# Eight modulation blocks moved from the input projection's VectorE sums to column matmuls between the RWKV projections' matmuls, and the RWKV stage's PSUM banks reordered

## The chip, the cores and the metric

One core of a Trainium2 chip runs the whole kernel. Its engines are TensorE (PE in the rows; its weight loads are shown apart as PEld), VectorE (DVE), ScalarE (ACT), GpSimd (POOL) and SyncE (SP), which issues the transfers. Each engine runs its own program in order. The metric is the time of one execution in microseconds. The time before is 3966.14 us, the median of three runs (3945.2 to 3976.5).

## The reference, cut to what matters

A trunk of two layers works on 128 context tokens and 1024 latent tokens (1152 in all, D_MODEL 1024, float32). Each layer modulates a normalised input by a conditioning vector, projects it once for four mixers of 512 channels each, and projects their outputs back.

```python
def reference(...):
    for l in range(DEPTH):                       # for the context with c_ctx, for the latents with c
        mod = silu(c) @ w_mod[l] + b_mod[l]      # 3 * 1024 values: shift, scale, gate
        x = trunk_layer(x, mod, ...)
    y = rmsnorm(x, final_g)

def trunk_layer(x, mod, p, states, rows, rope):
    shift, scale, gate = split(mod, 3)
    h = rmsnorm(x, norm_g) * (1 + scale) + shift
    u_a, u_b, u_c, u_d = split(h @ w_in, SPLITS)
    y_a, y_b, y_c = mlstm_branch(u_a), rglru_branch(u_b), retention_branch(u_c)
    y_d = rwkv_branch(u_d)
    y = concatenate([y_a, y_b, y_c, y_d]) @ w_out
    return x + gate * y

def rwkv step(s, r, w, k, v, kk, bb):            # per head, both directions over the tokens
    s = s * w + (s @ -kk) bb^T + v k^T
    return s, s @ r
```

## The kernel before

**Stages.** Per layer: the input projection `in_proj` with three mixers (mLSTM, RG-LRU, retention) running beside it, then the RWKV stage `rw_all`, then `tail` (the last output projection, the norm of the next layer). In the profile of before they lie at 61 to 1105 us and 1151 to 1990 us for layer 0, and at 2029 to 3013 us and 3060 to 3919 us for layer 1.

**Modulation.** `mod` of one layer is 24 columns of 128 values for two tokens' conditions, in six blocks of 512 values. The first four blocks of layer 0 are made in the opening norm. The other eight (`MODS`, line 1461) are made by `modulation` (line 1109), which `in_proj` of layer 0 steps through once every few projection jobs (lines 1263 to 1273). A block loads eight 128x512 tiles `wmod`, and VectorE multiplies each by one scalar per row and adds it to `macc`, for two conditions: 16 instructions a block, 128 in all. Then eight matmuls with a column of ones sum `macc` over the partitions into a bank that the projection also uses (`pmain`), and one small VectorE instruction adds the bias. Layer 1's `in_proj` steps through none.

**The RWKV stage.** Nine units (two per channel pair, and one for the context after the sixth) each take a *period* of `rw_all` (lines 162 to 295): `rw_chain`, 16 steps in which PE and VectorE alternate on one state, in `gap` 0 to 15; beside it VectorE runs `solve(n+1)`, 62 instructions that invert small triangular blocks, whose operands and result go through DRAM (`dU`, `iU`, `dN`, `SC<-dN`); after the chain comes `mid(n+1)`, matmuls that build the next unit's operands from the solved blocks. Ahead of the first period lies a prologue: `early(0)` (decay and gate vectors, sums over heads `v<-sq`, `v<-rk`), `operands(0)`, `scores(0)` (`a<-AR,BK`, masked into `SC`), `solve(0)`, `tokens(0)`, the same up to `scores(1)` for unit 1, `drain(1)`, `mid(0)`.

**Fills.** In both prologue and periods, PE gets other matmuls between the dependent ones: the 648 `fill` matmuls of `late_proj` (RWKV's own projections of pairs 1 to 3) and `out_proj` (line 1312, `main<-yt,ow`, 128x384). `pull(x)` (line 297) adds x to a credit and takes that many; `weave(g, x)` pulls x after each step of g; `drain(1)` takes what is left of the first 96. Each fill weight tile `ow` is 256 KB and comes from a ring of `OWB` = 6 buffers. PE keeps the program order of this stage (`strict`); the other engines' orders come from the scheduler by level. SP issues the loads of the ring and the solve's transfers in one order.

**PSUM.** The stage opens the pool `mo` (two banks, for fills) first and then `rw_ps` (six banks: tag `a` two, tags `v` and `u` two each).

Of the kernel before, what the change touches and what calls it, by code (L numbers as in the profile page):

```python
# [9 lines left out]
F32 = mybir.dt.float32  # L10
# [20 lines left out]
class B:  # L31
# [130 lines left out]
    def rw_all(self, l):  # L162
# [64 lines left out]
        def weave(g, x):  # L227
            for _ in g:
                self.pull(x)
# [3 lines left out]
        weave(early(0, 3), 8)  # L233
        operands(0, 3)
        weave(scores(0, 3), 3)
        solve(0)
        weave(tokens(0), 3)
# [8 lines left out]
        for n, (p, su) in enumerate(units):  # L246
# [6 lines left out]
            for gap in range(16):  # L253
                with self.level(3):
                    next(steps)
                self.pull(rate)
                if gap == 1 and finish is not None:
                    with self.level(1):
                        self.rw_gate(finish)
                        self.rw_final(l, finish)  # L260
                    self.finished += 1
                    finish = None
                if gap == 1 and n + 1 == N:
                    with self.level(1):
                        self.rw_gate(P[p])
                if gap >= 2:
                    next(tok, None)
                if gap == 4 and n + 2 < N:
                    block(n + 2)
                    pre = early(n + 2)  # L270
                if gap in (12, 14):
                    next(pre, None)
            weave(tok, 0)
# [23 lines left out]
    def pull(self, x):  # L297

        self.credit += x
        while self.credit >= 1:  # L300
            self.credit -= 1
            next(self.fills, None)

# [805 lines left out]
    def modulation(self, l, j, pool):  # L1109


        acc = [pool.tile([128, 512], F32, tag="macc%d" % e, name="macc") for e in range(2)]
        for k in range(8):
            w = pool.tile([128, 512], F32, tag="wmod", name="wmod", bufs=2)
            self.dma(w, self.i["w_mod"][l, j][:, k])
            for e in range(2):
                if k == 0:
                    self.ts(self.v, acc[e], w, self.sc[:, k, e:e + 1], MUL)
                else:
                    self.stt(self.v, acc[e], w, self.sc[:, k, e:e + 1], acc[e], MUL, ADD)  # L1120
        yield
        ps = self.pmain()[:, 0:8].rearrange("p (i c) -> p i c", c=2)
        for i in range(4):
            for e in range(2):
                self.mm(ps[:, i, e:e + 1], acc[e][:, 128 * i:128 * i + 128], self.ones[:, 0:1])
        self.tt(self.v, self.mod[l][:, 4 * j:4 * j + 4], ps,
                self.par["bmod"][:, 24 * l + 4 * j:24 * l + 4 * j + 4, None].broadcast_to([128, 4, 2]), ADD)
# [133 lines left out]
    def in_proj(self, l, wp, sp, mp, hh, hl):  # L1261
        n = 0
        mods = [self.modulation(z, j, mp) for z, j in MODS] if l == 0 else []
# [3 lines left out]
        for t_, (kind, name, p, tiles) in enumerate(JOBS):  # L1267
            if name[:3] == "rw_" and p in LATE:
                continue
            if mods and t_ % 4 == 0:  # L1270
                next(mods[0])
            if mods and t_ % 4 == 3:
                next(mods.pop(0), None)
# [101 lines left out]
    def build(self):  # L1375
# [10 lines left out]
        for l in range(2):  # L1386
# [7 lines left out]
            with self.ph as ph:  # L1394
                P = lambda n, b=1, **kw: ph.enter_context(tc.tile_pool(name=n + "_%d" % l, bufs=b, **kw, **tw))
                wp, sp = P("w"), P("st")
                self.in_proj(l, wp, sp, P("md") if l == 0 else None, *self.h)
# [26 lines left out]
            with ExitStack() as ph:  # L1424
                P = lambda n, b=1, **kw: ph.enter_context(tc.tile_pool(name=n + "_%d" % l, bufs=b, **kw, **tw))
                self.mainps = P("mo", 2, space=PSUM)
                wp, yp, sp = P("wo", OWB), P("yo", YOB), P("so", SO)
                with tc.high_priority(offset=HP1):
                    self.rl, self.rp = P("rw_lora", **R), P("rw_pair", **R)
                    self.rt, self.rd = P("rw_tmp"), (P("rw_even"), P("rw_odd", **R))  # L1430
                    self.rps = P("rw_ps", space=PSUM)
                    self.rw_layer(l, self.load_cols(self.rl, l, ("mu", "w0", "a0", "kk", "ka", "rk"), "rw_"))
# [11 lines left out]
                self.nfill = 648  # L1444
                self.rw_all(l)
# [15 lines left out]
MODS = ((0, 4), (0, 5), (1, 0), (1, 1), (1, 2), (1, 3), (1, 4), (1, 5))  # L1461
# [164 lines left out]
```

## Time and profile before

| what | value |
|---|---|
| median of 3 runs | 3966.14 us |
| the profiled execution, its time | 3965.97 us |
| its span | 3964.1 us |
[...]
| PE busy | 3624.5 us (91%) |
| DVE busy | 2110.8 us (53%) |
| ACT, POOL busy | 1290.7 us, 1119.5 us |
| transfers | 538 MB, mean 136 GB/s |

Times in rows are microseconds from the span's start. A matmul of float32 shows as two rows ("passes") in the trace, so 648 fills are 1296 rows a layer. An "[idle before <-X]" is the time for which the engine had nothing to run, and what ended it.

### The profile page before, as it was taken

What the parts mean: (1) busy time and instruction counts of PE and PEld (TensorE: products, weight loads), DVE (VectorE), ACT (ScalarE), POOL (GpSimd) and SP (SyncE); (2) the same over time, 40 slices, a digit from 0 to 9 for tenths busy, and PEclk for the clock granted to TensorE, in tenths of its full rate; (3) what the DMA queues carried; (4) which work ended last, traced back from release to release, by engine and by line L of the source; (5) the groups of instructions that cost most, each with busy time, mean ns of one, the idle gap of its engine ahead of it and who ended that gap; (6) DMA issues with size and microseconds to landing.
All of it is one profiled execution on the core that took longest, in us unless ns stands there. A gap on an engine that the chain in (4) does not pass through costs nothing. (4 is left out here: it accounts for less than half of the span.)

```text
span 3964.1 us, 69608 instructions
## 1 busy us (share of the span) xinstructions
PE 3624.5 (91%) x28018; PEld 2850.2 (72%) x28018; DVE 2110.8 (53%) x4081; ACT 1290.7 (33%) x2094; POOL 1119.5 (28%) x1016
## 2 busy tenths in 40 slices
PE   5898999999978999899888999999998889988997
PEld 2897888999955656555568898999996555555554
DVE  6555656433336576667264545443423556776644
ACT  3233342212222343343142344322222234343313
POOL 4222323453331122211033232344243312122200
PEclk7898898999979999899989899999897999999999
DMA  6545354434335454434663343434333444434446
GB/s 229 147 119 138 114 151 135 136 122 136 121 99 156 132 162 112 116 120 127 186 210 112 105 136 122 127 119 144 109 122 127 131 148 137 134 104 121 125 138 201
DMA packets 413549, 538.00 MB, mean 136 GB/s; under 512 B 141708, under 2 KB 322700, under 8 KB 413228
## 3 DMA queue, kind: packets, MB, share of 16 engines
q1 hardware_dynamic: 413228, 533.57, 44.7%
q8 instruction: 220, 3.60, 0.4%
q14 instruction: 101, 0.83, 0.1%
HBM read 387.17 MB, written 146.25 MB: 135 GB/s over the span
## 5 line engine op out<-in xcount | busy, mean ns | idle before, releaser
L1312 PE MATMUL main<-yt,ow 128*128 128x384 f32 x2592 | 990.5, 520 | 21.3 <-DVE xi L48 17.4
L1312 PEld LDWEIGHTS main<-yt,ow 128*128 128x128 f32 x2592 | 476.0, 197 | 316.6 <-issue 45.5
L59 PE MATMUL main<-hh,wring_h 128*128 128x384 f32 x1824 | 654.7, 359 | 22.8 <-ACT hh L56 9.8
L59 PE MATMUL main<-hl,wring_h 128*128 128x384 f32 x1824 | 648.1, 355 | 20.2 <-DVE hl L44 17.6
L59 PE MATMUL main<-hh,wring_l 128*128 128x384 f32 x1824 | 647.7, 355 | 0.0
L44 POOL TENSOR_TENSOR wring_l<-raw,wring_h 128x1024 fp32r<-128x1024 f32 x100 | 249.9, 2504 | 571.2 <-ACT wring_h L1258 428.9
L59 PEld LDWEIGHTS main<-hh,wring_h 128*128 128x128 f32 x1824 | 363.1, 199 | 38.5 <-ACT hh L56 10.3
L59 PEld LDWEIGHTS main<-hl,wring_h 128*128 128x128 f32 x1824 | 362.9, 199 | 33.6 <-DVE hl L44 21.5
L59 PEld LDWEIGHTS main<-hh,wring_l 128*128 128x128 f32 x1824 | 362.6, 199 | 8.2 <-issue 2.0
L59 PE MATMUL main<-wring_h,hh 128*128 128x256 f32 x864 | 265.0, 307 | 25.7 <-DVE st L1306 25.0
L59 PE MATMUL main<-wring_l,hh 128*128 128x256 f32 x864 | 261.0, 302 | 0.0
L59 PE MATMUL main<-wring_h,hl 128*128 128x256 f32 x864 | 259.2, 300 | 0.0
L44 DVE TENSOR_TENSOR iN<-iN,tm 64x31 f32<-64x31 f32 (+15 forms) x558 | 201.5, 361 | 15.4
L44 DVE TENSOR_TENSOR tm<-iU,iN 64x31 f32<-64x31 f32 (+15 forms) x558 | 201.1, 360 | 15.1
L1306 DVE COPY st<-main 128x384 f32<-128x384 f32 (+1 forms) x168 | 85.8, 511 | 219.8 <-PE main L59 178.4
L59 PEld LDWEIGHTS main<-wring_h,hh 128*128 128x128 f32 x864 | 178.0, 206 | 32.0 <-DVE st L1306 26.1
L44 POOL TENSOR_TENSOR t<-s_k,bb 128x512 f32<-128x512 f32 x36 | 63.3, 1758 | 465.7 <-ACT bb L56 465.7
L59 PEld LDWEIGHTS main<-wring_h,hl 128*128 128x128 f32 x864 | 177.6, 206 | 4.0 <-issue 1.1
L59 PEld LDWEIGHTS main<-wring_l,hh 128*128 128x128 f32 x864 | 177.7, 206 | 2.7
L1258 ACT CAST wring_h<-raw 128x1024 fp32r<-128x1024 f32 x100 | 103.4, 1045 | 199.7 <-PE main L59 174.4
L1304 ACT COPY st<-main 128x384 f32<-128x384 f32 (+1 forms) x168 | 73.6, 438 | 270.6 <-PE main L59 259.9
L56 ACT ACT_TABLE_LOAD x123 | 157.8, 1283 | 3.0 <-PEq L1618 0.7
(331 smaller groups left out, 6104.0 us busy)
## 6 DMA issues: line engine op xcount, KB each, us to landing
raw<-in_w_in SPq DMA_DIRECT2D x100, 512.0 KB, 4.1
ow<-in_w_in SPq DMA_DIRECT2D x144, 256.0 KB, 3.6
ow<-in_w_out SPq DMA_DIRECT2D x144, 256.0 KB, 2.7
yt<-h SPq DMA_DIRECT2D x144, 192.0 KB, 4.5
mrb<-mlrow SPq DMA_DIRECT2D x48, 384.0 KB, 4.1
x<-xi SPq DMA_DIRECT2D x96, 192.0 KB, 2.9
yt<-y SPq DMA_DIRECT2D x90, 192.0 KB, 3.2
wmod<-in_w_mod SPq DMA_DIRECT2D x64, 256.0 KB, 3.7
```

Source lines behind the costliest of these rows:

```text
L44: return e.tensor_tensor(out=out, in0=a, in1=b, op=op)
L56: return self.a.activation(out=out, in_=a, func=f, scale=scale, bias=bias)
L59: return self.t.matmul(out, l, r, start=start, stop=stop)
L1258: self.a.copy(hi, raw)
L1304: self.a.copy(q[:, :w], ps[:, :w])
L1306: self.v.tensor_copy(q[:, :w], ps[:, :w])
L1312: return self.pe(self.t.matmul(*a, **k))
```

## The change

**The modulation.** `in_proj` of layer 0 steps through no modulation any more, and its pool for `wmod` and `macc` is gone. In layer 0's RWKV stage, in four of the nine periods (1, 3, 6 and 7), `modulation` makes two blocks: each 128x128 piece of `wmod` is the stationary operand, the two conditions' `silu_c` (128x2) are the moving one, and PE accumulates over the eight k in one PSUM tile of tag `v`. That is 64 matmuls a period, 256 in all. From gap 4 on each fill that is pulled is followed by two of them; what is left runs after gap 15. Two small VectorE instructions a period add the bias. The tiles `wmod` take buffers of the ring `ow`.

**The prologue, in both layers.** No fills are woven into `early(0)` (before 8 a step), one a step into `scores(0)` (before 3), and 20 are pulled after `solve(0)`.

**The banks.** `mo` is opened behind `rw_ps`: `rw_ps` takes banks 0 to 5 and `mo` banks 6 and 7.

```diff
@@ rw_all
-        weave(early(0, 3), 8)
+        weave(early(0, 3), 0)
         operands(0, 3)
-        weave(scores(0, 3), 3)
+        weave(scores(0, 3), 1)
         solve(0)
+        self.pull(20)
         weave(tokens(0), 3)
...
+                if gap == 4 and l == 0 and n in MODS:
+                    self.beside = self.modulation(MODS[n], self.wp)
+            for _ in self.beside:
+                pass
             weave(tok, 0)
@@ pull
             next(self.fills, None)
+            next(self.beside, None)
@@ modulation
-    def modulation(self, l, j, pool):
-        acc = [pool.tile([128, 512], F32, tag="macc%d" % e, name="macc") for e in range(2)]
...
+    def modulation(self, blocks, pool):
+        ps = self.pst2("v")[:, :, 0:8].rearrange("p b (i c) -> p b i c", c=2)
         for k in range(8):
...
+            for z, (l, j) in enumerate(blocks):
+                w = pool.tile([128, 1, 512], F32, tag="ow", name="wmod")
+                self.dma(w, self.i["w_mod"][l, j][:, k:k + 1])
+                for i in range(4):
+                    self.pm(ps[:, z, i], w[:, 0, 128 * i:128 * i + 128], self.sc[:, k], start=(k + i == 0), stop=(4 * k + i == 31))
+                    if i % 2:
+                        yield
...
@@ in_proj
-        mods = [self.modulation(z, j, mp) for z, j in MODS] if l == 0 else []
...
-            if mods and t_ % 4 == 0:
-                next(mods[0])
-            if mods and t_ % 4 == 3:
-                next(mods.pop(0), None)
@@ build
-                self.mainps = P("mo", 2, space=PSUM)
                 wp, yp, sp = P("wo", OWB), P("yo", YOB), P("so", SO)
...
                     self.rps = P("rw_ps", space=PSUM)
+                    self.mainps = P("mo", 2, space=PSUM)
@@ numbers
-MODS = ((0, 4), (0, 5), (1, 0), (1, 1), (1, 2), (1, 3), (1, 4), (1, 5))
+MODS = {1: ((0, 4), (0, 5)), 3: ((1, 0), (1, 1)), 6: ((1, 2), (1, 3)), 7: ((1, 4), (1, 5))}
```

**PE in the prologue.** Before, PE's program in layer 0's prologue runs from the second `lora` step through the head sums and the first scores like this:

```order
L59 MATMUL a<-lora_x,lora_w 128x512 x2
L59 MATMUL v<-sq,bones 128x512
L1312 MATMUL main<-yt,ow 128x384 x8
L59 MATMUL v<-rk,bones 128x512 x2
L59 MATMUL a<-AR,BK 128x128 x8
L1312 MATMUL main<-yt,ow 128x384 x3
L59 MATMUL a<-AR,BK 128x128 x8
L1312 MATMUL main<-yt,ow 128x384 x3
L59 MATMUL a<-AR,BK 128x128 x8
```

In the change the same stretch reads as follows, up to the fourth group of scores and the fills behind it:

```order
L59 MATMUL a<-lora_x,lora_w 128x512 x2
L59 MATMUL v<-sq,bones 128x512
L59 MATMUL v<-rk,bones 128x512 x2
L59 MATMUL a<-AR,BK 128x128 x8
L1310 MATMUL main<-yt,ow 128x384
L59 MATMUL a<-AR,BK 128x128 x8
L1310 MATMUL main<-yt,ow 128x384
L59 MATMUL a<-AR,BK 128x128 x8
L1310 MATMUL main<-yt,ow 128x384
L59 MATMUL a<-AR,BK 128x128 x8
L1310 MATMUL main<-yt,ow 128x384 x21
```

The 16 fills of the two `early` steps (eight stand just ahead of the first row as well) and six of the nine between the scores are gone from here; 21 stand behind the last scores. The last stretch of fills, ahead of `mid(0)`, has 29 now and had 25.

**DVE at the end of `solve(1)`.** VectorE runs the solve's pairs (`tm`, `iN`) and, among them, `mid(0)`'s copies out of PSUM (`UV<-u`), on which the chain's first step waits. Before, the end of `solve(1)` reads:

```order
L44 TENSOR_TENSOR tm<-iU,iN 64x156
L44 TENSOR_TENSOR iN<-iN,tm 64x6x26
L582 COPY UV<-u 64x4x128
L44 TENSOR_TENSOR tm<-iU,iN 64x135
L44 TENSOR_TENSOR iN<-iN,tm 64x5x27
L44 TENSOR_TENSOR tm<-iU,iN 64x112
L582 COPY UV<-u 64x4x128
L44 TENSOR_TENSOR iN<-iN,tm 64x4x28
```

In the change the same part of VectorE's program is:

```order
L44 TENSOR_TENSOR iN<-iN,tm 64x4x28
L44 TENSOR_TENSOR tm<-iU,iN 64x87
L44 TENSOR_TENSOR iN<-iN,tm 64x3x29
L44 TENSOR_TENSOR tm<-iU,iN 64x60
L44 TENSOR_TENSOR iN<-iN,tm 64x2x30
L44 TENSOR_TENSOR tm<-iU,iN 64x31
L44 TENSOR_TENSOR iN<-iN,tm 64x31
L588 COPY UV<-u 64x4x128 x2
```

Both copies stand behind the solve's last instruction now; ten and seven of its instructions stood behind them before.

**PE in a period with modulation.** In the change, PE's program in gaps 4 to 6 of period 1 is this (in before the fills there stand three together):

```order
L1310 MATMUL main<-yt,ow 128x384
L59 MATMUL v<-silu_c,wmod 128x2 x2
L59 MATMUL a<-UV,SC 64x64 x16
L59 MATMUL u<-ST,AR 64x64 x4
L1310 MATMUL main<-yt,ow 128x384
L59 MATMUL v<-silu_c,wmod 128x2 x2
L1310 MATMUL main<-yt,ow 128x384
L59 MATMUL v<-silu_c,wmod 128x2 x2
L62 MATMUL a<-ident,BK 128x128 x4
L59 MATMUL u<-UV,BT 64x64 x4
```

The `x2` are two of the 256 new matmuls, with no instruction of the chain moved past another.

## Rows read from the trace of the kernel before

**Rows 1.** The page: busy time of each engine over the span.
```profile
PE 3624.5 (91%) x28018; PEld 2850.2 (72%) x28018; DVE 2110.8 (53%) x4081; ACT 1290.7 (33%) x2094; POOL 1119.5 (28%) x1016
```

**Rows 2.** The first and last projection matmul of each layer, by start, in the timeline.
```profile
60.60 0.69 PE L59 MATMUL main<-hh,wring_h 128*128 128x384 f32 x1 [6.09 <-ACT hh L56]
...
1103.09 0.33 PE L59 MATMUL main<-hh,wring_h 128*128 128x384 f32 x1
...
2028.91 0.34 PE L59 MATMUL main<-hh,wring_h 128*128 128x384 f32 x1
...
3012.86 0.33 PE L59 MATMUL main<-hh,wring_h 128*128 128x384 f32 x1
```

**Rows 3.** Busy time by engine between them; after POOL: clock, DMA share, GB/s.
```profile
60.60:1103.10 1042.50, 974.31 (x5674) 911.33 (x5675) 533.56 (x798) 309.22 (x447) 381.06 (x350) 0.90 0.44 131
2028.90:3012.90 984.00, 937.28 (x5561) 877.14 (x5561) 445.79 (x665) 317.32 (x460) 361.77 (x348) 0.94 0.42 124
```

**Rows 4.** The tile macc: duration in ns (least, median, most), starts.
```profile
L59 PE MATMUL main<-ones,macc x128: 166/250/353, 128.0 to 834.9; 128*128 128x1 f32 x128
L48 DVE SCALAR_TENSOR_TENSOR macc<-wmod,silu_c,macc x112: 730/746/2866, 39.7 to 765.9; 128x512 f32<-128x512 f32 x112
```

**Rows 5.** The timeline around the opening norm's last steps on DVE.
```profile
55.48 1.40 DVE L48 SCALAR_TENSOR_TENSOR macc<-wmod,silu_c,macc 128x512 f32<-128x512 f32 x2
56.80 0.17 DVE L52 TENSOR_SCALAR sg<-mod 128x16 f32<-128x16 f32 x1
```

**Rows 6.** One block's ones matmuls, and fills in period 6, in PE's timeline.
```profile
127.97 1.84 PE L59 MATMUL main<-ones,macc 128*128 128x1 f32 x16
...
1800.23 2.20 PE L1312 MATMUL main<-yt,ow 128*128 128x384 f32 x6
1802.36 0.34 PE L59 MATMUL u<-ST,AR 64*64 64x64 f32 x8
```

**Rows 7.** The page: the fills' matmuls and weight loads in both layers.
```profile
L1312 PE MATMUL main<-yt,ow 128*128 128x384 f32 x2592 | 990.5, 520 | 21.3 <-DVE xi L48 17.4
L1312 PEld LDWEIGHTS main<-yt,ow 128*128 128x128 f32 x2592 | 476.0, 197 | 316.6 <-issue 45.5
```

**Rows 8.** Chains of periods 1, 3, 6 and 7 as stretches, columns of rows 3.
```profile
1355.90:1414.40 58.50, 56.95 (x498) 35.51 (x494) 39.71 (x108) 19.64 (x36) 8.49 (x7) 0.94 0.47 136
...
sum 224.80, PE 218.87 PEld 136.21 DVE 161.15 ACT 81.54 POOL 33.33; mean PE 54.72 PEld 34.05 DVE 40.29 ACT 20.39 POOL 8.33
```

**Rows 9.** PE's timeline right behind the chain of period 6.
```profile
1818.58 0.45 PE L59 MATMUL v<-ident,SC 32*32 32x32 f32 x4 [1.03 <-DMA SC<-dN]
1821.07 0.24 PE L59 MATMUL v<-ident,SC 32*32 32x32 f32 x2 [2.04 <-DMA SC<-dN]
```

**Rows 10.** SP's timeline late in period 1, and the page's line on wmod.
```profile
1399.99 0.33 SPq L81 DMA_DIRECT2D dN<-iN  x1
...
1403.87 3.78 SPq L81 DMA_DIRECT2D SC<-dN  x8
...
wmod<-in_w_mod SPq DMA_DIRECT2D x64, 256.0 KB, 3.7
```

**Rows 11.** PE's timeline in the prologues, layer 0 and (last row) layer 1.
```profile
1155.04 5.77 PE L1312 MATMUL main<-yt,ow 128*128 128x384 f32 x16
...
1161.81 1.12 PE L59 MATMUL v<-sq,bones 128*128 128x512 f32 x2
...
1174.91 0.79 PE L59 MATMUL a<-AR,BK 64*128 64x128 f32 x2 [2.06 <-POOL BK L44]
...
1284.16 0.49 PE L59 MATMUL u<-ST,AR 64*64 64x64 f32 x8 [10.14 <-DVE UV L582]
...
3192.96 0.49 PE L59 MATMUL u<-ST,AR 64*64 64x64 f32 x8 [9.32 <-DVE UV L582]
```

**Rows 12.** DVE's timeline at solve(1), layer 0.
```profile
1260.00 0.91 DVE L514 MEMSET iN<- 64x1024 f32 x1 [13.49 <-ACT iU L513]
...
1283.32 0.69 DVE L582 COPY UV<-u 64x512 f32<-64x512 f32 x1
```

More of the change, by code (lines that the diff above doesn't have):

```diff
@@ L1107, in mod_rows @@
                 self.par["bmod"][:, 24 * l + 4 * j:24 * l + 4 * j + 4, None].broadcast_to([128, 4, 2]), ADD)
-    def modulation(self, l, j, pool):
-        acc = [pool.tile([128, 512], F32, tag="macc%d" % e, name="macc") for e in range(2)]
+    def modulation(self, blocks, pool):
+        ps = self.pst2("v")[:, :, 0:8].rearrange("p b (i c) -> p b i c", c=2)
         for k in range(8):
[L1114 to L1127, printed above, removed]
+            for z, (l, j) in enumerate(blocks):
[5 more added lines that the diff above has]
+                        yield
+        for z, (l, j) in enumerate(blocks):
+            self.tt(self.v, self.mod[l][:, 4 * j:4 * j + 4], ps[:, z],
+                    self.par["bmod"][:, 24 * l + 4 * j:24 * l + 4 * j + 4, None].broadcast_to([128, 4, 2]), ADD)
     def modulation0(self, pool, ps, between):
@@ L1259, in split_w, with in_proj @@
         self.tt(self.g, lo, raw, hi.bitcast(F32), SUB)
-    def in_proj(self, l, wp, sp, mp, hh, hl):
+    def in_proj(self, l, wp, sp, hh, hl):
         n = 0
-        mods = [self.modulation(z, j, mp) for z, j in MODS] if l == 0 else []
         rh = wp.tile([128, 3, KT, 128], F32R, name="wring_h")
@@ L1396, in build @@
                 wp, sp = P("w"), P("st")
-                self.in_proj(l, wp, sp, P("md") if l == 0 else None, *self.h)
+                self.in_proj(l, wp, sp, *self.h)
                 with tc.high_priority(offset=HP1), ExitStack() as st:
@@ L1444, in build @@
                 self.nfill = 648
+                self.beside, self.wp = iter(()), wp
                 self.rw_all(l)
```

## The prediction

> **What bounds the kernel now.** I read the page first, then the stretches of each stage, then the timeline where the change touches it. PE is busy 3624.5 us of the 3964.1 [rows 1], so in nearly every stage work that leaves PE or a wait that ends on PE is worth its length, and work on another engine is worth only what PE waits for it. What the reader should see next is that the kernel brings its own control for the largest part of the change. `in_proj` runs twice on the same shapes, with modulation beside it in layer 0 and without it in layer 1. From the first projection matmul to the last, layer 0 needs 1103.09 − 60.60 = 1042.5 us, and layer 1 needs 3012.86 − 2028.91 = 984.0 us [rows 2]. So the same projection and the same three mixers cost 58.5 us more where the modulation runs.
>
> The busy times say where the 58.5 us lie [rows 3]. DVE is busy 87.8 us more in layer 0 (533.56 against 445.79), and the 16 instructions a block explain it: 112 of them take 746 ns each in the median, some far more [rows 4]. PE is busy 37.0 us more (974.31 against 937.28), and idle 21.5 us more (68.2 against 46.7). Of the 37.0 us, 128 passes with a column of ones at 1.84/16 = 0.115 us [rows 6] are 14.7 us; I give the rest to the clock, whose mean grant is 0.90 against 0.94 [rows 3].
>
> The RWKV stage is the other place. Its periods 1, 3, 6 and 7, into which the modulation goes, have chains of 224.8 us together, and PE is busy in 218.9 us of them [rows 8]. There are 5.9 us in which added PE work could disappear.
>
> **Part 1, what in_proj gives back.** The PE order of layer 0's projection in the change is that of its layer 1, apart from a few per mille of the instructions, and every mixer's instruction stands where layer 1 of before has it, within a few places. So I take layer 1 as the forecast for layer 0: −58 us. Bounds: −45, if some 13 of the 22 us (37.0 − 14.7) by which layer 0's PE is busy longer without the passes have another cause and stay; −66, if the bank that the ones matmuls held had cost a little more in layer 0 than layer 1 shows. In the opening norm the last `macc` pair ends only as `sg`, on which the first projection waits, starts at 56.80 [rows 5]; that pair's 1.4 us go too: −1, at most −5 for the pairs ahead of it.
>
> **Part 2, the column matmuls.** 256 matmuls are 512 passes, each with a new 128x128 weight tile and two columns streamed. The nearest row is the ones matmul: same weight tile, one column, 0.115 us a pass [rows 6]. 512 × 0.115 = 59 us; start to start inside the run is nearer 0.112, hence +57. From above: 0.250 us, the median duration of one such pass [rows 4], gives 128 us, but that duration overlaps with its neighbours', so I take it as no more than an outer end and use 70 (a fill's own wait on the weight that follows). From below: a fill's weight load takes 197 ns, and all of them lie beneath 520 ns matmuls [rows 7]; between two fills one of four new loads can lie beneath the fill ahead and one fill's load beneath the new ones, so a quarter may vanish: +43.
>
> The row says that the pass is bound by loading its weights. [...]
>
> What hides of the +57: the 5.9 us of idle time in the four chains [rows 8], and 3.1 us behind period 6, where `mid` waits for the solved blocks `SC<-dN` [rows 9], which a longer chain makes ready in time. I take −7 of these 9.
>
> Then new waits. The 64 loads of 256 KB move with the work. Each takes one of six ring buffers which the fills' weights had alone; a load landed in 3.7 us [rows 10]. In a period the ring now turns over about 26 tiles (16 `wmod`, some 10 `ow`) in some 72 us, 2.8 us each, so six buffers look about 14 us ahead, enough for 3.7. But SP issues in order: in the change, nine of period 1's 16 `wmod` loads stand ahead of the solve's result `dN<-iN` and seven behind it and behind the eight `SC<-dN`. In before, those were issued at 1399.99 and until 1407.65, that is 44 to 52 us after the chain began at 1355.9 [rows 8, 10]. The tenth tile would land near 1408 + 3.7, 56 us after the start. PE reaches that tile in gap 12: 13 of the 16 gaps, about 44 of the 58.5 us, and 18 pairs of new matmuls ahead of it (18 × 0.45 = 8 us) make 52 us after the start. The solve may end a little earlier because fewer chain steps are mixed into it now. So I expect some 2 us of waiting in each of four periods: +8. Bounds 0, and +35 if each of the seven late loads of each period costs PE about 1.2 us.
>
> The eight small additions on DVE count as nothing: layer 0's `out_proj` and `tail` read `mod` periods later, and PE waits for none of them.
>
> **Part 3, the prologues.** The fills leave `early(0)`. Before, 16 passes (5.77 us) stood between the two `lora` steps, so the second `v<-sq` came at 1161.81; the branch through ACT, DVE and POOL to the first `a<-AR,BK` then took until 1174.91, 13.1 us [rows 11]. Without the fills that branch starts about 5 us earlier, at 1157, and AR,BK at about 1170. But PE now has nothing in these 13 us except three pairs of head sums (3.4 us), and one fill between the scores where there were three: it idles some 9 us there. By `drain(1)` the same 96 fills must be done in both kernels, so PE reaches the end of the drain later by the added idle time, about 8 us. Of that, four fills' worth (8 passes at 0.36 us [rows 6], 2.9 us) have moved behind `scores(1)`, which so comes 5 us later.
>
> The chain starts with `u<-ST,AR`, which waits 10.14 us for a copy `UV<-u` on DVE [rows 11]. This is what ends last, not PE's fills: DVE had waited 13.49 us for the solve's operands until 1260.00, and the copy at 1283.32 stands among the solve's last instructions [rows 12]. Solve(1) follows scores(1), so the 5 us reach it in full. And both copies now stand behind all of the solve, ten and seven instructions later, about 2 us. So the chain starts 7 us later. Layer 1's prologue has the same wait, 9.32 us [rows 11], and the same edit. Both: +14. From below: if the earlier scores(0) also let everything behind it come earlier, the 5 us of fills return and it is 0. From above, if nothing starts earlier for want of fills, PE idles 13.1 − 3.4 us and some 1.4 us between each two scores, 14 a layer: +28.
>
> **Part 4, the banks.** The first PE instructions of the stage stand behind the same nine retention transposes as before, and no instruction changes its place. 0; the retention's last reads, which release the banks, cover it. Uncovered it would be one fill's wait, about a microsecond a layer.
>
> **The sum.** −58 − 1 + 57 − 7 + 8 + 14 + 0 = +13 us, against the profiled execution's 3965.97 us: 3979. That execution is within 0.2 us of the median of the runs, 3966.14, so it stands for both.
>
> **The rivals.**
>
> *The column matmuls hide, faster.* If a pass with two columns slides beneath its neighbours, as all the fills' weight loads do [rows 7], the 512 passes cost little more than a quarter, 15 us, and the sum is −29: 3937. With prologues that cost nothing, −43: 3923. For it: the fills' weight loads overlap. Against it: the run of 16 ones passes at 0.115 us, where the streaming was as short as here and nothing overlapped [rows 6]. Chance 0.15, of which 0.1 beyond 3926, where the prologues help too. [...]
>
> *SP's order holds the ring, slower.* If PE comes to the tenth `wmod` tile with its load still behind `SC<-dN`, it stops, the chain's step behind it stops, and every later fill waits for a ring buffer too. The point from which it decides: the solve's result issued later than some 45 us after the chain's start, about where it stands now (44) [rows 8, 10]. The price: in each of the four periods the wait until landing, up to 8 us, plus a landing of 3.7 us less 1.9 us of work for six further tiles, 11 us; 4 × 19 − 8 = 68 more than I count, at worst 3979 + 68 = 4047; half of it 4013. For it: loads on one queue with a wait for DVE ahead. Against it: 3.7 us to land, and the solve has fewer chain steps in it. Chance 0.2 for over 4006.
>
> *Nothing moves.* −58 and +57 cancel, the ring keeps up and the prologues cost nothing: 3966 − 9 = 3957. This lies in my range and within 1%. Chance 0.2; my forecast as summed, 0.45.
>
> **How the numbers follow.** 1% is 40 us, about what a measurement of this kernel can tell from no change (its three runs lie 31 us apart). The forecast and "nothing moves" are within 1%; so is half of the slower rival's beginning. Faster by over 1% (below 3926) 0.1, plus 0.02 for a larger gain in `in_proj` than its control shows: 0.12. Slower by over 1% (above 4006): 0.2. Within: 0.68. All lower bounds together are −66 − 5 + 43 − 9 = −37, all upper ones −45 − 1 + 70 − 4 + 35 + 28 = +83: 3929 to 4049. The range leaves out the outer part of the two rivals, a tenth on either side: 3940 to 4022. The likeliest case alone is 3960 to 3995.
>
> **What would show it.** In the profile after: layer 0's projection should take 984 ± 6 us from first to last matmul, with DVE busy near 446 us in it. Periods 1, 3, 6 and 7 should be 12 to 17 us longer and the other five the same; pairs `v<-silu_c,wmod` should stand 0.45 us a pair. Waits of PE for `wmod` in the timeline beyond 10 us in total would show the SP rival, passes under 0.06 us the faster one. `u<-ST,AR` of each layer should start 5 to 9 us later after the stage's first `lora`, still behind a `UV` copy; if it starts earlier, my step on DVE's order is wrong.

## The result

The changed kernel takes 3995.59 us, the median of seven runs (3988.65 to 4006.41), against 3960.91 us of before in the same count (3945.2 to 3976.5). The ratio is 1.0098 with a 95% interval of 1.0073 to 1.0124: 1% slower, 35 us, at the edge of what the prediction called "within 1%". The time lies inside the prediction's range of 3940 to 4022 us and 17 us above its 3979, but its sum of +13 us was too small by more than half of what came.

The profile of the change has a span of 4001.0 us, at a mean granted clock of 0.924 of full speed (0.923 in before's). Its busy line, beside [rows 1]:

```profile
PE 3674.1 (92%) x28402; PEld 2895.8 (72%) x28402; DVE 2000.3 (50%) x3953; ACT 1290.3 (32%) x2094; POOL 1096.0 (27%) x1016
```

PE gained 50 us of busy time, and DVE lost 110. The first and last projection matmul of each layer, in PE's timeline of the change, answer to [rows 2]:

```profile
56.45 0.69 PE L59 MATMUL main<-hh,wring_h 128*128 128x384 f32 x1 [4.04 <-ACT hh L56]
...
1045.00 0.33 PE L59 MATMUL main<-hh,wring_h 128*128 128x384 f32 x1
...
2076.72 0.63 PE L59 MATMUL main<-hh,wring_h 128*128 128x384 f32 x1
...
3044.83 0.33 PE L59 MATMUL main<-hh,wring_h 128*128 128x384 f32 x1
```

The busy times of (nearly) these two stretches, columns as in [rows 3]: span, PE, PEld, DVE, ACT, POOL, granted clock, DMA share, GB/s.

```profile
56.45:1046.70 990.25, 936.21 (x5560) 877.22 (x5560) 443.94 (x674) 308.86 (x448) 365.21 (x350) 0.93 0.40 123
2076.70:3046.50 969.80, 934.75 (x5596) 875.58 (x5595) 438.98 (x682) 318.88 (x466) 361.86 (x349) 0.95 0.41 127
```

And the chains of periods 1, 3, 6 and 7 as stretches, beside [rows 8]:

```profile
1299.00:1388.00 89.00, 84.99 (x625) 60.74 (x622) 41.38 (x114) 21.11 (x40) 12.09 (x12) 0.79 0.45 137
1483.70:1562.00 78.30, 72.61 (x626) 51.52 (x622) 43.12 (x116) 19.78 (x37) 9.31 (x8) 0.93 0.51 150
1759.30:1838.50 79.20, 77.74 (x576) 55.30 (x572) 44.55 (x110) 26.64 (x50) 14.13 (x14) 0.87 0.56 169
1852.40:1933.80 81.40, 76.42 (x630) 56.40 (x626) 40.65 (x110) 18.13 (x28) 5.75 (x4) 0.87 0.48 142
sum 327.90, PE 311.77 PEld 223.95 DVE 169.69 ACT 85.67 POOL 41.27; mean PE 77.94 PEld 55.99 DVE 42.42 ACT 21.42 POOL 10.32
```

The four chains take 327.9 us where they took 224.8: +103.1 us. Cut at these and a few more marks of PE's timelines (first `lora`, last chain matmul), the two profiled executions differ like this:

| stretch | before, us | change, us | difference | forecast |
|---|---|---|---|---|
| to the first projection matmul | 60.6 | 56.5 | −4.1 | −1 |
| projection of layer 0, first to last | 1042.5 | 988.6 | −53.9 | −58 |
| RWKV of layer 0, first `lora` to last chain matmul | 807.0 | 904.8 | +97.8 | +65 |
| from there to layer 1's first projection matmul | 71.2 | 78.3 | +7.1 | 0 |
| projection of layer 1, first to last | 984.0 | 968.1 | −15.9 | 0 |
| first `lora` of layer 1 to the end | 903.9 | 907.7 | +3.8 | +7 |
| the two stretches between projection and `lora` | 95.0 | 97.1 | +2.1 | 0 |

They add up to +36.9 us, the difference of the spans. So the step on `in_proj` came out, the step on the column matmuls was too small by a third of what came, and layer 1's projection, which the prediction had at zero, came out shorter. Each column is one execution, and layer 1's projection differs by up to 27 us between kernels with one and the same PE order (below).

**Where the 103 us come from.** In period 1 fills and pairs of column matmuls follow each other like this, at first and later (PE's timeline of the change; its first row is an earlier wait):

```profile
1303.30 1.70 PE L59 MATMUL a<-AR,BK 64*128 64x128 f32 x16 [1.49 <-DVE SC L44]
...
1321.69 0.89 PE L1310 MATMUL main<-yt,ow 128*128 128x384 f32 x2
1322.42 0.50 PE L59 MATMUL v<-silu_c,wmod 128*128 128x2 f32 x4
1322.78 0.89 PE L1310 MATMUL main<-yt,ow 128*128 128x384 f32 x2
...
1350.96 0.61 PE L59 MATMUL v<-silu_c,wmod 128*128 128x2 f32 x4 [2.46 <-DMA wmod<-in_w_mod]
...
1367.06 1.65 PE L1310 MATMUL main<-yt,ow 128*128 128x384 f32 x2
1368.50 0.85 PE L59 MATMUL v<-silu_c,wmod 128*128 128x2 f32 x4
1369.21 1.63 PE L1310 MATMUL main<-yt,ow 128*128 128x384 f32 x2
```

From fill to fill it is 1.09 us at first, of which the fill alone would take 0.71 [rows 6]. Between the two stands a wait of 2.46 us for a `wmod` load, and behind it fill to fill is 2.15 us. Two stretches of the same length, ahead of the wait and behind it, say why:

```profile
1321.30:1350.90 29.60, 27.20 (x245) 20.84 (x243) 17.56 (x55) 8.48 (x15) 0.00 (x0) 1.00 0.54 158
1352.00:1381.60 29.60, 29.60 (x98) 19.99 (x97) 7.77 (x14) 5.74 (x11) 5.72 (x5) 0.51 0.38 125
```

The granted clock is 1.00 ahead of the wait and 0.51 behind it, and PE is busy there without a gap. In all the lower clock stays for 34 us, past the modulation's last pass. Behind the 1.49 us wait at 1303.30, among scores and fills, it was gone after some 3 us (0.50 from 1305 to 1308 us, 1.00 from 1309). The other three periods have one wait for `wmod` each (PE's timeline of the change):

```profile
1537.82 0.61 PE L59 MATMUL v<-silu_c,wmod 128*128 128x2 f32 x4 [2.06 <-DMA wmod<-in_w_mod]
...
1816.35 0.64 PE L59 MATMUL v<-silu_c,wmod 128*128 128x2 f32 x4 [1.46 <-DMA wmod<-in_w_mod]
...
1910.26 0.61 PE L59 MATMUL v<-silu_c,wmod 128*128 128x2 f32 x4 [2.23 <-DMA wmod<-in_w_mod]
```

Behind these waits stand three stretches at the lower clock. The second row here is the rest of period 3's modulation:

```profile
1540.30:1547.10 6.80, 6.80 (x26) 3.98 (x25) 0.65 (x3) 1.27 (x2) 0.00 (x0) 0.50 0.25 77
1547.20:1557.80 10.60, 10.60 (x67) 7.76 (x66) 6.49 (x11) 3.13 (x6) 3.96 (x4) 1.00 0.50 161
1816.80:1837.20 20.40, 20.40 (x118) 14.75 (x119) 7.71 (x16) 3.04 (x7) 8.10 (x8) 0.50 0.62 196
1912.40:1932.80 20.40, 20.40 (x155) 16.46 (x154) 1.29 (x6) 0.00 (x0) 0.00 (x0) 0.50 0.34 101
```

They last 7, 20 and 20 us, which makes 82 us in the four periods. In period 3 the clock was back while two-column passes still ran, behind a group of `lora` matmuls of 512 columns; in periods 1 and 6 such a group did not bring it back, so what ends the lower clock is not shown. Nor does every wait of this size bring it: period 2's chain, without modulation, has waits of 1.51 and 1.60 us for VectorE at a clock of 1.00. At the lower clock, fill to fill takes twice as long (2.15 us against 1.09), so half of the 82 us is lost, 41 us. The waits are 8.2 us. The 54 us that are left of the 103 are near the 57 that the prediction had for the passes.

### The profile page after: what moved, and what is told of

Its sections match the earlier page's. It is cut to its first block, busy times and chain, and to the rows that moved or that the text cites. A ratio compares the mean times of both kernels' runs of the same rounds, so it can differ in the third digit from the quotient of the medians.

```text
span 4001.0 us, 70206 instructions
## 1 busy us (share of the span) xinstructions
PE 3674.1 (92%) x28402; PEld 2895.8 (72%) x28402; DVE 2000.3 (50%) x3953; ACT 1290.3 (32%) x2094; POOL 1096.0 (27%) x1016
## 5 line engine op out<-in xcount | busy, mean ns | idle before, releaser
L1310 PE MATMUL main<-yt,ow 128*128 128x384 f32 x2592 | 1027.5, 530 | 23.6 <-DVE xi L48 20.3
L44 DVE TENSOR_TENSOR tm<-iU,iN 64x31 f32<-64x31 f32 (+15 forms) x558 | 197.7, 354 | 15.9
L44 DVE TENSOR_TENSOR iN<-iN,tm 64x31 f32<-64x31 f32 (+15 forms) x558 | 193.7, 347 | 16.1
```

Source lines behind the costliest of these rows:

```text
L44: return e.tensor_tensor(out=out, in0=a, in1=b, op=op)
L1310: return self.pe(self.t.matmul(*a, **k))
```

## The experiments

The theory after this reading: the waits for `wmod` are as small as forecast, but each makes the clock fall, and the thin passes (those with two columns) that follow keep it down until the modulation of that period ends; period 3 fits this only in part. All runs, against the runs of before on the same chip:

| kernel | median, us | ratio to before | 95% interval |
|---|---|---|---|
| modulation alone | 4006.7 | 1.0108 | 1.0060 to 1.0156 |
| prologues alone | 3988.2 | 1.0065 | 1.0043 to 1.0087 |
| banks alone | 3958.8 | 0.9986 | 0.9969 to 1.0003 |
| prologues and banks | 3972.1 | 1.0036 | 1.0018 to 1.0055 |
| the change without the modulation's work | 3911.9 | 0.9872 | 0.9823 to 0.9921 |
| the change, 128 columns a pass | 3968.8 | 1.0024 | 1.0002 to 1.0046 |
| the change, one block a period | 3978.3 | 1.0054 | 1.0032 to 1.0077 |
| the change, periods 0, 2, 4, 5 | 4020.9 | 1.0167 | 1.0127 to 1.0207 |
| 128 columns, prologues of before, banks last | 3954.2 | 0.9980 | 0.9964 to 0.9996 |
| the same, blocks spread to period 8 | 3950.9 | 0.9984 | 0.9964 to 1.0004 |

### The three parts alone

Modulation alone, with the old prologues and bank order:

```diff
-        weave(early(0, 3), 0)
+        weave(early(0, 3), 8)
...
-        weave(scores(0, 3), 1)
+        weave(scores(0, 3), 3)
         solve(0)
-        self.pull(20)
...
+                self.mainps = P("mo", 2, space=PSUM)
                 wp, yp, sp = P("wo", OWB), P("yo", YOB), P("so", SO)
...
-                    self.mainps = P("mo", 2, space=PSUM)
```

> Only the modulation moves, as in the change; the prologues keep 8 and 3 fills a step and the fills' banks stay first. Theory (the column matmuls cost some 52 us of passes, 8 us of waits for wmod behind the solve's transfers, and some 40 us because PE's granted clock falls behind each of these waits and stays low; prologues and banks cost about nothing): the time is that of the whole change, 3985 to 4005 us, and chains 1, 3, 6 and 7 take 78 to 89 us each. Rival (a part of the 40 us comes from the bank order or the prologue's fills, which shift what stands in those periods): 3950 to 3980 us, with these chains near 70 us.

It is 1.08% slower, as the whole change or more. A part of that is a wait in layer 1's projection (read under the next run), so the chains say more: they take 72.8, 92.1, 78.0 and 84.3 us, 327.2 us in all against 327.9 in the change, with two of them outside the 78 to 89 us. So neither the bank order nor the prologues make the 40 us. One of its periods is a control that nobody planned. In period 1 PE waited only 0.45 us for `wmod` in this run, and in period 3 it waited 3.61 us. PE's timeline at both:

```profile
1353.94 0.61 PE L59 MATMUL v<-silu_c,wmod 128*128 128x2 f32 x4 [0.45 <-DMA wmod<-in_w_mod]
...
1525.27 0.61 PE L59 MATMUL v<-silu_c,wmod 128*128 128x2 f32 x4 [3.61 <-DMA wmod<-in_w_mod]
```

The modulation's whole stretch in period 1, and the stretch behind the wait in period 3, as windows with the granted clock after POOL:

```profile
1323.80:1368.10 44.30, 43.85 (x355) 32.83 (x353) 25.00 (x69) 13.31 (x24) 3.95 (x4) 1.00 0.64 191
1526.20:1555.90 29.70, 29.70 (x97) 19.92 (x98) 8.60 (x16) 5.26 (x10) 5.60 (x5) 0.51 0.29 89
```

In period 1 the clock stayed at 1.00 through all 128 thin passes, and the chain took 72.8 us, 14.3 more than before: the price that the prediction had for one period (57/4). In period 3 it was 92 us. So the passes as such did not lower the clock; with a wait of 3.61 us among them it fell to 0.51.

The prologues alone:

```diff
-        weave(early(0, 3), 8)
+        weave(early(0, 3), 0)
...
-        weave(scores(0, 3), 3)
+        weave(scores(0, 3), 1)
         solve(0)
+        self.pull(20)
```

> Only the prologues change (no fills in early(0), one a step in scores(0), 20 behind solve(0)), in both layers; modulation and banks as before. The prediction's step: +14 us, the chain of each layer starting 7 us later. Theory now: the chain starts 6 us later but its first period is 4 to 6 us shorter, since the solve no longer stands among the chain's first steps on DVE; +3 us in all, -3 to +8.

26 us slower in paired runs by ratio (the interval is 17 to 34), more than either forecast, and the profile puts little of it in the prologues: from the first `lora` to the end of the first chain 192.7 us against 191.0 in layer 0, 192.3 against 189.9 in layer 1. But layer 1's projection takes 1009.2 us where it took 985.6 (to the last projection pass), and a wait stands in it that before does not have:

```profile
2348.80 0.69 PE L59 MATMUL mup<-mV,mkw 128*128 128x65 f32 x2 [6.69 <-DMA mV<-ut_ml_vo]
```

The kernel with the modulation alone has layer 1's projection in the same PE order instruction by instruction, and there too PE waits 6.78 us at this place, with 17 us at the lower clock behind it, in a projection of 1002.8 us. None of the other kernels here has that order or that wait.

The banks alone:

```diff
-                self.mainps = P("mo", 2, space=PSUM)
                 wp, yp, sp = P("wo", OWB), P("yo", YOB), P("so", SO)
...
                     self.rps = P("rw_ps", space=PSUM)
+                    self.mainps = P("mo", 2, space=PSUM)
```

> Only the bank order changes: rw_ps in banks 0 to 5, the fills' pool in 6 and 7. The prediction's step: 0 us. Rival: layer 0's stretch from the last chain matmul to layer 1's first projection matmul, 71.2 us before and 78.3 us in the change, is longer by some 7 us because of the banks, and the time is 5 to 10 us above before.

No difference that can be told from zero. The rival on layer 0's tail is not borne out by the time, though that stretch is 76.7 us here; it is 74.9 to 81.0 us in every variant, those with the old bank order too, so 71.2 us in before's one profile says little. What the banks do is elsewhere: with them last, PE's order in layer 1's projection is another one than in before.

### Prologues and banks together

Both of the last two diffs.

> The prologue and the bank order of the change together, with the modulation as before. Theory: the prologue alone cost 26 us almost wholly in layer 1's input projection, where PE comes to mup before its reloaded operand (a wait of 6.7 us and 17 us of half clock in its profile); with the banks last the scheduler puts mup some 22 projection matmuls later there, the wait is gone, and the time is that of before: 3955 to 3972 us. Rival (the cost is the prologue's own, in its own stage): 3980 to 3990 us.

3972 us, at the upper end of the theory's range. Layer 1's projection takes 977.4 us, and the wait for `mV` is gone. The time is 16 us below the prologues alone by medians, which come from two chips, and 11 us by the ratios to before (1.0036 against 1.0065), whose intervals overlap. So by the ratios some 11 of the 26 us went with the wait, less than half. Between this kernel and the banks alone there remain 13 us by medians and 20 by ratios (1.0036 against 0.9986) that no single stretch shows.

The reason that the expectation gave falls, too. In the trace `mup` stands at projection matmul 1210 of the layer with the wait and at 1206 to 1212 in the runs without it, not 22 earlier; what differs is the load, which landed 12 us after its issue where 7.5 us or less sufficed in before (issued at 2326.3, `mup` at 2333.8 without a wait). Why it took so long stays open. Layer 1's projection alone varies from 967.6 us (the kernel with 128 columns a pass) to 994.4 us (one block a period) between kernels with one and the same PE order. The granted clock makes most of that: 21 of the 27 us are PE's busy time for the same matmuls, at a mean clock of 0.96 in the shorter and 0.93 in the longer.

### The change without the modulation's work

```diff
                 if gap == 4 and l == 0 and n in MODS:
-                    self.beside = self.modulation(MODS[n], self.wp)
+                    for l_, j_ in MODS[n]:
+                        self.v.tensor_copy(self.mod[l_][:, 4 * j_:4 * j_ + 4], self.par["bmod"][:, 24 * l_ + 4 * j_:24 * l_ + 4 * j_ + 4, None].broadcast_to([128, 4, 2]))
```

> The change without its column matmuls and without their 64 loads; the eight blocks of the modulation then hold the bias alone, so that part of the computation is left out. By the theory (the modulation costs about 100 us in the four periods) 3895 us, 3885 to 3910. By the prediction's price (57 us of passes, 8 of waits, 7 hidden) 3938 us. Chains 1, 3, 6 and 7 should be those of before, 55 to 59 us each.

3912 us by median: between the two forecasts and nearer to the theory's. The chains take 58.5, 60.1, 57.2 and 56.2 us, 232 us in all, so the modulation's work adds 96 us to them. In time, the modulation in the four periods costs 3995.6 − 3911.9 = 84 us by medians, or 1.0098 − 0.9872 = 0.0226 of 3961, 90 us, by the ratios. The prediction's price was 58 (57 − 7 + 8).

### More columns in the same passes

The moving operand is read 64 times over (stride zero), so that each pass streams 128 columns in place of two; weights, loads, places on PE and the count of passes stay.

```diff
-        ps = self.pst2("v")[:, :, 0:8].rearrange("p b (i c) -> p b i c", c=2)
+        ps = self.pst2("v").rearrange("p b (i x c) -> p b i x c", x=64, c=2)
...
-                    self.pm(ps[:, z, i], w[:, 0, 128 * i:128 * i + 128], self.sc[:, k], start=...)
+                    self.pm(ps[:, z, i], w[:, 0, 128 * i:128 * i + 128], self.sc[:, k, None].broadcast_to([128, 64, 2]), start=...)
...
-            self.tt(self.v, self.mod[l][:, 4 * j:4 * j + 4], ps[:, z],
+            self.tt(self.v, self.mod[l][:, 4 * j:4 * j + 4], ps[:, z, :, 0],
```

> The change, but each column matmul streams its two conditions 64 times over (128 columns into 128 PSUM columns, of which two are read): same weights, same loads, same places on PE and SP. Theory (a wait for wmod makes the granted clock fall, and the thin passes that follow keep it down to the end of the modulation): the waits of 1.5 to 2.5 us stay, the clock is back within some 7 us behind them, a pass still costs its weight load, and chains 1, 3, 6 and 7 take 70 to 78 us: 3955 to 3975 us. Rival (the clock stays low for as long whatever streams, or the wider passes cost more than they give back): 3990 us or more, half clock for 20 us and more behind each wait.

27 us below the change, though each pass does 64 times the streaming. PE's timeline of this kernel in period 1, ahead of the wait and behind it:

```profile
1323.88 0.81 PE L1310 MATMUL main<-yt,ow 128*128 128x384 f32 x2
1324.53 0.61 PE L59 MATMUL v<-silu_c,wmod 128*128 128x128 f32 x4
1324.97 0.81 PE L1310 MATMUL main<-yt,ow 128*128 128x384 f32 x2
...
1352.77 0.71 PE L59 MATMUL v<-silu_c,wmod 128*128 128x128 f32 x4 [1.76 <-DMA wmod<-in_w_mod]
1353.41 0.35 PE L59 MATMUL u<-ST,AR 64*64 64x64 f32 x8
1353.68 1.55 PE L1310 MATMUL main<-yt,ow 128*128 128x384 f32 x2
1355.03 1.06 PE L59 MATMUL v<-silu_c,wmod 128*128 128x128 f32 x4
1355.88 1.48 PE L1310 MATMUL main<-yt,ow 128*128 128x384 f32 x2
1357.16 0.65 PE L59 MATMUL v<-silu_c,wmod 128*128 128x128 f32 x4
1357.65 0.81 PE L1310 MATMUL main<-yt,ow 128*128 128x384 f32 x2
```

From fill to fill it is 1.09 us, as with two columns, (1.09 − 0.71)/4 = 0.095 us for each pass: the streaming adds nothing that shows. Behind a wait of 1.76 us the clock falls here too, but it is back some 4 us later, with the fill at 0.81 us again. The four chains as stretches:

```profile
1300.90:1376.00 75.10, 71.73 (x624) 51.25 (x620) 41.60 (x114) 21.09 (x40) 8.59 (x8) 0.95 0.55 164
1473.30:1550.10 76.80, 70.20 (x625) 50.20 (x620) 43.23 (x118) 19.76 (x37) 8.63 (x8) 0.98 0.52 153
1744.60:1816.30 71.70, 69.66 (x576) 49.00 (x570) 44.80 (x110) 26.63 (x50) 12.54 (x11) 1.00 0.62 187
1830.20:1904.60 74.40, 68.17 (x630) 49.39 (x624) 40.52 (x110) 18.12 (x28) 5.75 (x4) 1.00 0.54 155
sum 298.00, PE 279.76 PEld 199.83 DVE 170.15 ACT 85.59 POOL 35.51; mean PE 69.94 PEld 49.96 DVE 42.54 ACT 21.40 POOL 8.88
```

298.0 us against 327.9 of the change, with clocks of 0.95 to 1.00 against 0.79 to 0.93. PE waits for loads a little longer in all (1.76, 3.14, 2.04 and 3.02 us in the four, the last two in pieces of at most 1.05 and 1.71 us). Behind these waits the lower clock came in periods 1 and 3 alone, for 3.4 us each, 7 us where the change had 82. So the waits by themselves did not cost the 41 us; it took passes that stream only two columns. The run changes the passes ahead of a wait as well as those behind it, so it does not tell whether the thin passes only kept the clock down, as in the theory, or also helped it to fall. What remains above before, 73 us, is passes and waits, close to the prediction's 57 + 8.

### One block a period

```diff
-MODS = {1: ((0, 4), (0, 5)), 3: ((1, 0), (1, 1)), 6: ((1, 2), (1, 3)), 7: ((1, 4), (1, 5))}
+MODS = {1: ((0, 4),), 2: ((0, 5),), 3: ((1, 0),), 4: ((1, 1),), 5: ((1, 2),), 6: ((1, 3),), 7: ((1, 4),), 8: ((1, 5),)}
```

> The change with one block of modulation in each of the periods 1 to 8 in place of two in 1, 3, 6 and 7: the same matmuls and loads in all, eight loads a period. Theory: nearly all loads now stand ahead of the solve's transfers on SP, PE waits less than 1 us for wmod in most periods, the clock does not fall there, and the modulation costs some 50 us less what idle time it finds in periods 2, 4 and 5: 3940 to 3965 us. Rival (the thin passes lower the clock without any wait): 3985 to 4000 us as in the change.

3978 us: faster than the change, slower than expected, and both halves of that can be read. In periods 1, 3, 6 and 7 PE waited for no `wmod`, the clock did not fall at the modulation, and the chains took 63.6, 67.9, 61.4 and 62.6 us, 31 us in all above before for four blocks. In periods 2, 4 and 5 the new matmuls do not start on time, and for a reason the expectation had left out: PE stands at them and at the head sums ahead of them, which want the same PSUM tag `v`.

```profile
1399.10 1.13 PE L59 MATMUL v<-sq,bones 128*128 128x512 f32 x2 [1.83 <-DVE rn L52]
1401.01 2.03 PE L59 MATMUL v<-rk,bones 128*128 128x512 f32 x2 [0.78 <-DVE rn L52]
1403.82 2.08 PE L59 MATMUL v<-rk,bones 128*128 128x512 f32 x2 [0.78 <-DVE bs L44]
1406.68 1.01 PE L59 MATMUL v<-silu_c,wmod 128*128 128x2 f32 x4 [0.78 <-DVE bs L44]
```

These head sums (`block(n + 2)` makes them where a new pair begins) stand in periods that the change avoids. The clock then falls ahead of the thin passes (two passes of `v<-rk` take 2.03 and 2.08 us in these rows, two of `v<-sq` 1.13) and stays down for up to 30 us (chain 2: 88.9 us against 65.2).

### The periods with idle time

```diff
-MODS = {1: ((0, 4), (0, 5)), 3: ((1, 0), (1, 1)), 6: ((1, 2), (1, 3)), 7: ((1, 4), (1, 5))}
+MODS = {0: ((0, 4), (0, 5)), 2: ((1, 0), (1, 1)), 4: ((1, 2), (1, 3)), 5: ((1, 4), (1, 5))}
```

> The change with its two blocks a period in periods 0, 2, 4 and 5, whose chains left PE idle for 11.0, 3.9, 10.2 and 6.9 us before, in place of 1, 3, 6 and 7. Theory: up to 20 us of the passes hide in that idle time, but the loads still stand behind the solve's transfers, so the waits and the lower clock behind them remain in some periods: 3965 to 3990 us. Rival (the idle time is not usable, since the chain waits for DVE and the added passes only make its next step later): 3995 us as the change.

4021 us, the slowest of all, beyond both forecasts. These are the same head-sum periods, now with twice the passes in them: the chain of period 4 takes 122.8 us (78.3 before), with 24 us at the lower clock from the head sums on, a 3.86 us wait for `wmod`, and 48 us more at the lower clock behind it. Here the idle time of a chain was no room for thin passes: it sits among waits, and the clock fell at these.

### Two better versions

With 128 columns a pass, the banks last and the old prologues (the edit against the kernel with 128 columns):

```diff
-        weave(early(0, 3), 0)
+        weave(early(0, 3), 8)
...
-        weave(scores(0, 3), 1)
+        weave(scores(0, 3), 3)
         solve(0)
-        self.pull(20)
```

> The change with 128 streamed columns a pass, as in e_wide, and with the prologues of before (8 and 3 fills a step); the fills' banks stay last. Theory (the prologue costs 10 to 20 us also with the banks last, as the pair of runs with and without it showed: 3972 against 3959 us): e_wide's 3969 us less that, 3948 to 3960 us, level with before or a little faster. Rival (the prologue costs nothing once the banks are last, and what those two runs differ by is chance): 3964 to 3972 us.

3954 us, 0.2% faster than before with an interval that just leaves out 1, and 15 us below the kernel with the new prologues: the theory's case, so the new prologues cost some 15 us even with the banks last (17 by the ratios). Then with the blocks spread (the edit against the last one):

```diff
-MODS = {1: ((0, 4), (0, 5)), 3: ((1, 0), (1, 1)), 6: ((1, 2), (1, 3)), 7: ((1, 4), (1, 5))}
+MODS = {1: ((0, 4), (0, 5)), 3: ((1, 0),), 6: ((1, 1),), 7: ((1, 2), (1, 3)), 8: ((1, 4), (1, 5))}
```

> As e_wide_old, with one block of modulation in periods 3 and 6, and the two freed blocks in period 8, behind which no solve stands: {1: 2, 3: 1, 6: 1, 7: 2, 8: 2} blocks. Theory: with eight loads a period PE waited for no wmod in periods 3 and 6, and in period 8 no solve holds SP, so some 4 us of waits go: 3942 to 3956 us. Rival (period 8 has no slack and ends the stage, so its passes come out in full while the waits were worth nothing): 3952 to 3962 us.

3951 us, not to be told from the last one. Periods 3 and 6 showed no wait for `wmod` (62.0 and 61.8 us), but period 8 got a wait of 2.76 us and 17 us more. So the theory's step for period 8 was wrong. The time lies in the theory's range and 1 us below the rival's; with an interval of 8 us to either side it decides nothing between them.

## Why the prediction was right or wrong, step by step

**in_proj (right).** −58 forecast, −53.9 measured, DVE 443.9 us busy against "near 446". Layer 1 of before was a good control for layer 0, and the other profiles agree: the stretch takes 1031.3 to 1042.5 us in the four kernels with the modulation beside it, and 972.8 to 992.0 us in the eight without, 55 us less on the mean. The start gave 4.1 us, inside its −1 to −5.

**The passes (right).** 57 us forecast, at 0.45 us a pair. At a clock of 1.00 a pair of matmuls costs 0.38 us in the rows above, 49 us for the 128 pairs. The one undisturbed period came out 14.3 us longer, 57 for four, with 2.1 us of it idle time. The faster rival, passes hidden beneath their neighbours, did not come: a pass costs 0.095 us with two columns and with 128. That the weight load bounds it is the prediction's reading; what the runs show is that 126 more columns added no time, and that weight loads are busy for 1.75 of the 1.84 us of the ones matmuls [rows 6] and for 1.31 of the 1.33 us of twelve column passes in a row (at 1556.53 in the change).

**The wait for wmod (right as a wait, wrong as a price).** The prediction had PE at the tenth tile 52 us into the chain of period 1, its load landing at 56, and about 2 us of waiting a period. SP's timeline of the change, for that period:

```profile
1340.43 0.42 SPq L81 DMA_DIRECT2D dN<-iN  x1
...
1344.02 3.78 SPq L81 DMA_DIRECT2D SC<-dN  x8
1347.90 0.88 SPq L81 DMA_DIRECT2D wmod<-in_w_mod  x2
```

The solve's result was issued 41.4 us into the chain, the first `wmod` behind the eight `SC<-dN` at 1347.90, and PE, there at 1348.50 or 49.5 us in, went on at 1350.96, 52 us in. Load and PE both came some 3 us earlier than forecast, so the wait held. (The working has a slip: thirteen of sixteen gaps are 47.5 of the 58.5 us, not 44, which would have left almost no wait.) The four waits sum to 8.2 us; the term was +8. **The step that failed is this term**, "some 2 us of waiting in each of four periods: +8": it priced a wait by its length. What it had to price was the wait and the clock behind it, 8 + 41 us, and so the four chains came out 23 to 31 us longer, not 12 to 17. The prediction named the clock once, as a part of layer 0's 37 us, and did not carry it to the place where it put a new wait among the least dense matmuls of the kernel. The rival on SP's order had the right place for the loss but a wrong price too: it counted on the ring being held, and the ring recovered after one wait.

**What hides (half right).** −7 forecast, from the chains' idle time and from the wait behind period 6. The second came: the waits of [rows 9] are gone, and from that chain's end to the next period's start it is 5.6 us less. The first did not: the chains' idle time is 327.9 − 311.8 = 16.1 us now against 5.9 [rows 8], the new 8.2 us and 2 us more.

**The prologues (wrong in their place).** Each chain was to start 7 us later. In the change it is this, to be read against [rows 11]:

```profile
1093.65 2.08 PE L59 MATMUL a<-lora_x,lora_w 64*128 64x512 f32 x4
...
1227.32 0.49 PE L59 MATMUL u<-ST,AR 64*64 64x64 f32 x8 [4.03 <-DVE UV L588]
```

From the first `lora` that is 133.7 us where it was 133.4; in layer 1 it is 135.2 against 132.7. The scores of unit 1 came 4 us later, near the 5 worked out, and the `UV` copies stand behind the whole solve. But the first scores came only 1.4 us earlier, not 5: from the second `v<-sq` to them it is 17.6 us now, and was 13.1. And "the 5 us reach it in full" was wrong: the solve's operands came back from DRAM sooner. From the last mask to the solve's copy on ACT it was 12.2 us before and 5.4 us in the change. Before, the last `dU<-SC` was issued 3.4 us after that mask, behind other loads on SP, and the copy came 5.3 us after the issue of `iN<-dU`; in the change the first is nothing and the second 2.3 us.

Measured alone the prologues cost more than forecast, 26 us. Some 11 of these went with the wait in layer 1's projection, which the prediction did not look at for this edit. In the two pairs of kernels with the banks last, 13 and 15 us remain by medians (20 and 17 by ratios). That is near the +14 of the sum, but the profiles show only some 3 us of it at the starts of the two chains, where the prediction had it all. So the agreement counts as luck, and where the rest of the time goes stays open.

**The banks (wrong in "no instruction changes its place").** They change PE's order in layer 1's projection. Alone that is within the noise; with the prologues some 11 us by the ratios go with it. Whether it made the −15.9 us in the table is not shown: to their last pass, the three kernels with the change's own order take 969.8, 976.7 and 981.5 us there against 985.6 in before, and kernels of one order spread by 27 us.

So it is in part luck that the range held, because errors of both signs lay inside it: +41 for the clock and +7 in layer 0's tail, against −16 in layer 1's projection and −11 in the two prologues.

## What to carry to other kernels

Price a wait on PE by what runs behind it: among scores and fills the lower clock was gone after some 3 us, among two-column passes it cost five times the waits themselves (41 us for 8.2). The small matmuls here took 126 extra columns at no cost (0.095 us a pass either way), and with these the lower clock behind the waits was down to 7 us in all. Before adding loads to a queue, look at which in-order wait stands ahead of them, and after any edit compare the orders of the stages that the edit does not touch.

## What the runs showed of the hardware

A pass with 128 columns of moving operand took no longer from start to start than one with two (1.09 us from fill to fill in both). In the change the granted clock fell behind single waits of 1.46 to 2.46 us among thin passes. It did not fall behind one of 0.45 us with the modulation alone, nor in the change behind waits of 1.51 and 1.60 us in a chain without such passes. Where it fell among them it stayed at 0.50 to 0.51 of full speed for 7 to 34 us while PE was busy without a gap. Where the passes streamed 128 columns it fell in two of four periods, for 3.4 us each. Thin passes slow down with it: twelve in a row took 1.40 us at the higher level (at 1556.53) and 2.56 us at the lower (at 1379.12).
